# A trunk layer on one core: the output projection by seven products of quarters instead of eight blocks

## The chip, the core and the metric

The kernel runs on one core of a Trainium2 chip. A core has engines that each work through an instruction queue of their own, in order: TensorE (PE, matrix products; its weight loads are shown apart as PEld), VectorE (DVE), ScalarE (ACT), GpSimd (POOL) and SyncE (SP), which here issues nearly all the DMA transfers. They wait for one another through semaphores. The metric is the device time of one execution in microseconds (us); a run's median over several executions is compared.

## The reference, cut to what matters

One pre-norm residual layer on x of 512 rows and 1024 columns: a token mixer of three gated branches (attention, pooling, a state-space scan), an output projection, and a gated feed-forward block. The lines around the change are these:

```python
merged = gates[:, :, 0] * y_a + gates[:, :, 1] * y_b + gates[:, :, 2] * y_c
x = x + merged @ w_o[i]
x = x + conv_ffn(rmsnorm(x, ln2_g[i]), ffn_w_up[i], ffn_conv_w[i], ffn_conv_b[i], ffn_w_down[i])
```

`y_c` ends in a product with `w_c`; `merged @ w_o` is a 512 x 1024 by 1024 x 1024 product; the norm of its residual sum feeds the up projection `u @ w_up`. All is float32.

## The kernel before

**Products in three passes.** A float32 operand is split into a high part that TensorE can take (a cast on ScalarE, `cast`, L196) and the rest (a subtraction on VectorE, `lows`, L216). `mm3` (L237) adds high x high, high x low and low x high into one PSUM bank. For weights the parts are `wh` and `wl`, 128 x 2048 each for a 1 MB piece of weights; a piece arrives by one DMA on SP's queue (`fetch`, L184, tile `raw`, two buffers).

**Jobs.** The program is a list of jobs, each with one piece of weights. When job n starts, its instructions are recorded in this order: the split of job n+1 on VectorE, the cast of job n+2 on ScalarE (spread in halves over the job's steps), the fetch of job n+3 on SP, and then the job's own products and what takes their results. Each engine runs its instructions in exactly this recorded order. `step()` is called within a job; it flushes spread halves and moves on generators that wait in `running` (small pieces of other work, such as the transposes of a norm).

**Around the output projection.** Four jobs multiply by `w_c` (`branch_jobs` with `last=True`), two column chunks each, 24 matmuls of 128 x 512 per chunk. After chunk m, VectorE multiplies the result by its gate (L1162) and adds it to the merged sum `MG[m]` (L1163), ScalarE casts the sum (L1166, `mgh`) and VectorE takes the rest (L1167, `mgl`): 128 of the 1024 merged columns, for all 512 rows, are then ready as an operand.

`wo_jobs` forms the output: for each pair of row blocks (0, 1 and 2, 3), for each half h of the output columns, two jobs of four k blocks each. A job has two blocks of 12 matmuls, one per row block; a pair and half accumulates over two jobs in the same banks. So w_o is fetched, cast and split twice, once per pair: eight jobs of 24 matmuls. After the second job `evac` adds the bank to x (`X1[tb, h]`, L1188). For h = 0 `norm_early` starts the second norm (squares on ScalarE, L440; a product with the norm weights on GpSimd, L464); for h = 1 `norm_late` ends it (L472 square root, L474 to L482), and `norm_turn` transposes the normalised rows on TensorE (L453), with a cast (L456) and a split (L457) into `uh`, `ul`. The last two row blocks' norms run beside the first two up jobs (`opening`, L1356): high and low products of the first 256 rows, then one row block's transposes, then the product with `wl`.

PSUM has eight banks of 128 x 512, four with the tag "mm" and four with "sm". The columns of the up projection's convolution weights (`ff_cols`, tile `fcol`) are turned by two small transposes in this region.

**Products of quarters** stand in the kernel already, for two projections of the first stage (`sevens`) and for the down projection (`down_group`). There the left operand is cut in row halves (`LO`, `HI`) and in even and odd k blocks, the weights in k and column quarters, and seven products with sums of quarters replace eight. `sums_of` (L326 to L336) makes the sums of a pair of operand blocks: four 128 x 256 operations on VectorE, two casts on ScalarE, two splits on VectorE. `diff` (L341) subtracts one 128 x 2048 piece of weights from another. Two buffers of a pool (tile `w`, tag "xs") hold two quarters of weights; the first down group's pair is fetched there early, at the start of the w_c stage.

Of the kernel before, what the change touches and what calls it, by code (L numbers as in the profile page):

```python
# [10 lines left out]
F32 = mybir.dt.float32  # L11
F32R = mybir.dt.float32r
AF = mybir.ActivationFunctionType
# [70 lines left out]
def trunk(ctx: ExitStack, tc, out, x, rel_bias, ln1_g, w_in, b_gate, w_a, pool_w, pool_scale, w_b,  # L84
# [80 lines left out]
    def after(n, it):  # L165
        for _ in range(n):
            yield
        yield from it
# [57 lines left out]
    def wsrc(w, k0, k1, c0, c1):  # L226
        return w[k0 * P:k1 * P, c0:c1].rearrange("(k p) c -> p k c", p=P)

    def mm3(ps, wh, wl, xh, xl, ks, first=True, last=True, flip=False, onto=False):


        first = first and not onto
        n, total = 0, 3 * len(ks)
        for a, b in ((wh, xh), (wh, xl), (wl, xh)):
            for k in ks:
                l, r = (b(k), a(k)) if flip else (a(k), b(k))
                pe.matmul(ps, l, r, start=first and n == 0, stop=last and n == total - 1,  # L237
                          skip_group_check=onto)
                n += 1
# [82 lines left out]
    def sums_of(f0, f1, ah, al, found):  # L322


        sa, sb = T("sa"), T("sb")
        dve.tensor_tensor(sa[:, LO], f0[:, HI], f1[:, HI], OP.add)  # L326
        dve.tensor_tensor(sa[:, HI], sa[:, LO], f0[:, LO], OP.subtract)
        dve.tensor_tensor(sb[:, LO], f0[:, LO], f0[:, HI], OP.subtract)
        dve.tensor_tensor(sb[:, HI], f1[:, LO], sa[:, HI], OP.subtract)
# [5 lines left out]
        dve.tensor_sub(al, sa, ah.bitcast(F32))  # L335
        dve.tensor_sub(bl, sb, bh.bitcast(F32))  # L336
        for j, h, l, half in ((1, ah, al, LO), (2, ah, al, HI), (3, bh, bl, LO), (4, bh, bl, HI)):
            found(j, h[:, half], l[:, half])
# [117 lines left out]
            act.copy(hh, pv)  # L456
            dve.tensor_sub(ul[:, 4 * h:4 * h + 4, tb * P:(tb + 1) * P], pv, hh.bitcast(F32))  # L457
# [10 lines left out]
    def norm_late(t, g, v0, outs, last=False):  # L468
# [3 lines left out]
        act.activation(sq, ss, AF.Sqrt, bias=v0, scale=1.0 / D)  # L472
        xg = T("xg")
        dve.tensor_tensor(xg, t, g[:, S:], OP.mult)  # L474
        dve.scalar_tensor_tensor(v, ss, 1.0 / D, v0, OP.mult, OP.add)
        yield xg
        dve.reciprocal(r, sq)
        dve.scalar_tensor_tensor(rt, r, v, r, OP.mult, OP.mult)
        dve.tensor_scalar(rt, rt, -0.5, 1.5, OP.mult, OP.add)
        if not last:  # L480
            for o, src in outs(xg):
                dve.tensor_scalar(o, src, r, rt, OP.mult, OP.mult)  # L482
# [672 lines left out]
    def branch_jobs(b, w, parts, nk, last=False, more=()):  # L1155
        def evac(m, ps):
            if b == 1:
                MG[m] = T("yo")
                act.copy(MG[m], ps)
                return  # L1160
            s = SG[b, m]
            dve.tensor_tensor(s, s, ps, OP.mult)  # L1162
            (dve if last else pool).tensor_tensor(MG[m], MG[m], s, OP.add)  # L1163
            if last:
                h, l = T("mgh", F32R), T("mgl", F32R)
                act.copy(h, MG[m])  # L1166
                dve.tensor_sub(l, MG[m], h.bitcast(F32))  # L1167
                MH[m] = (h, l)

        return jobs_a(w, 0, 8, lambda k: parts[k][0], lambda k: parts[k][1], nk, evac,  # L1170
                      width=256 if nk > 4 else 512, more=more)


    X1 = {}
# [7 lines left out]
                t = X1[tb, h] = T("x1")  # L1182
                sp.dma_start(t, x[tb * P:(tb + 1) * P, h * S:(h + 1) * S])

    def wo_jobs(pair, h):
        def evac(tb, ps):
            t = X1[tb, h]
            dve.tensor_tensor(t, t, ps, OP.add)  # L1188
            if h == 0:
                nxt[tb] = norm_early(t, nxt["g2"])  # L1190
                return
# [5 lines left out]
            it = norm_late(t, nxt["g2"], v0, lambda xg1: ((us[0], xg0), (us[1], xg1)))  # L1197
            next(it)

            def rest():  # L1200
                next(it, None)
                yield
                norm_turn(us, nxt["uh"], nxt["ul"], tb)

            if pair == 0:
                r = rest()
                next(r)
                running.append(after(1, r))
# [8 lines left out]
        return jobs_b(lambda k0, k1: [wsrc(w_o, k0, k1, h * S, h * S + S)], S,  # L1217
                      lambda k, tb: MH[k][0][:, tb * P:(tb + 1) * P],
                      lambda k, tb: MH[k][1][:, tb * P:(tb + 1) * P], KD, evac,
                      blocks=(2 * pair, 2 * pair + 1), turn_over=pair == 1 and h == 1)  # L1220


    ACTS = {}
# [171 lines left out]
    def early(tb):  # L1395
        yield
        fin[tb] = norm_early(X1[tb, 0], fin["g"])
# [25 lines left out]
    def program():  # L1423
# [33 lines left out]
            else:  # L1457
                yield Call(lambda i=int(token): waiting.append(y_norm(i)))
        yield Call(finish)
        yield from branch_jobs(2, w_c, YT, 8, last=True)  # L1460
        yield Call(load_x1)
        for pair in range(2):
            for h in range(2):
                yield from wo_jobs(pair, h)
            if pair == 0:
# [235 lines left out]
```

## Time and profile before

| | |
|---|---|
| median of 3 runs | 1033.1 us (1032.99 to 1033.64) |
| the profiled execution | 1032.69 us |
| its span in the profile | 1030.9 us |
| TensorE busy | 1019.8 us, 5276 matmuls |
| VectorE, ScalarE, GpSimd busy | 702.7, 490.2, 132.8 us |
| w_c product | from 583.0 us |
| output projection | 626.5 to 672.3 us |
| opening of the up projection | 672.3 to 685.8 us |

Times of rows are from the span's start. A row of a group gives line, engine, operation, output <- inputs by tile names, the shape and the count; then busy us and mean ns of one; then the idle time of the engine just before these instructions and what ended it. A row of the timeline gives the start, the length, the engine and the operation, with the idle time before it in brackets. A row of several merged instructions counts from the start of the first to the end of the last. In the trace the tiles `X1` are called `x`, and the banks of the projection `pb`.

### The profile page before, as it was taken

How to read it: one execution, taken by the hardware profiler on the slowest of the kernel's cores; microseconds unless marked ns; L12 is line 12 of the kernel's file. 1: busy time of each engine (PE TensorE's matmuls, PEld its weight loads, DVE VectorE, ACT ScalarE, POOL GpSimd, SP SyncE). 2: the span in 40 equal slices, each digit the busy share in tenths (PEclk: the TensorE clock that was granted, in tenths of full speed). 3: DMA queues.
4: the chain of work that ended last, by engine and by line, in shares of the span. 5: the costliest groups of instructions: out<-in, count | busy, mean ns of one | idle time of the engine just before them, and what ended most of it. 6: DMA issues, size and time to landing. Idle time of an engine off the chain costs nothing.

```text
span 1030.9 us, 13254 instructions
## 1 busy us (share of the span) xinstructions
PE 1019.8 (99%) x5276; PEld 858.0 (83%) x5276; DVE 702.7 (68%) x932; ACT 490.2 (48%) x784; POOL 132.8 (13%) x114
## 2 busy tenths in 40 slices
PE   8999999999999999999999999999999999999997
PEld 8998877899888887788888888898888888888885
DVE  6553566788756648666688856767778668685756
ACT  6432545454674363567575324545444434433434
POOL 1770000000000001100044501101111100111002
PEclk9999999999999999999999999999999999999999
DMA  8444312034322354551253625543232233421322
GB/s 270 135 129 137 108 57 75 31 88 138 123 82 82 93 158 108 133 144 44 80 151 128 203 82 203 171 142 121 82 122 83 84 117 112 138 82 41 123 82 82
DMA packets 113357, 117.62 MB, mean 114 GB/s; under 512 B 5236, under 2 KB 97207, under 8 KB 113296
## 3 DMA queue, kind: packets, MB, share of 16 engines
q1 hardware_dynamic: 112703, 115.92, 36.4%
q8 instruction: 41, 0.67, 0.3%
q10 hardware_dynamic: 592, 0.86, 0.2%
q14 instruction: 21, 0.16, 0.1%
HBM read 112.97 MB, written 2.22 MB: 112 GB/s over the span
## 4 chain that ended last, share of the span: by engine, by line
PE 91%; DVE 4%; ACT 3%; issue 1%; DMA 1%; ACTq 0%; DVEq 0%
PE pa L237 30%; PE pu L237 22%; PE pb L237 12%; PE pd L237 7%; PE pqk L237 6%; PE pa L1552 2%; PE pq L237 2%; PE pu L1356 1%; PE ps L743 1%; PE pt L772 1%; PE ppw L237 1%; PE po L784 1%; DVE xs L1133 1%; DVE wl L216 1%; PE py L1057 1%
## 5 line engine op out<-in xcount | busy, mean ns | idle before, releaser
L216 DVE TENSOR_TENSOR wl<-raw,wh 128x2048 fp32r<-128x2048 f32 (+3 forms) x95 | 220.3, 2320 | 53.3 <-ACT wh L196 43.5
L196 ACT CAST wh<-raw 128x1024 fp32r<-128x1024 f32 (+3 forms) x188 | 187.6, 1017 | 48.3 <-DVE raw L341 18.0
L1251 DVE SCALAR_TENSOR_TENSOR hc<-pu,fcol,hc 128x510 f32<-128x510 f32 x88 | 65.8, 748 | 56.0 <-ACT hc L1248 54.4
L237 PE MATMUL pa<-uh,wh 128*128 128x512 f32 x384 | 98.4, 398 | 0.0
L237 PE MATMUL pa<-ul,wh 128*128 128x512 f32 x384 | 94.9, 389 | 0.0
L237 PE MATMUL pa<-uh,wl 128*128 128x512 f32 x384 | 94.8, 389 | 0.0
L237 PEld LDWEIGHTS pa<-ul,wh 128*128 128x128 f32 x384 | 72.1, 188 | 15.1
L237 PEld LDWEIGHTS pa<-uh,wl 128*128 128x128 f32 x384 | 72.1, 188 | 15.0
L237 PE MATMUL pu<-uh,wh 128*128 128x512 f32 (+1 forms) x352 | 83.6, 379 | 0.0
L237 PE MATMUL pu<-uh,wl 128*128 128x512 f32 (+1 forms) x352 | 83.5, 379 | 0.0
L237 PE MATMUL pu<-ul,wh 128*128 128x512 f32 (+1 forms) x352 | 83.5, 379 | 0.0
L237 PEld LDWEIGHTS pa<-uh,wh 128*128 128x128 f32 x384 | 70.3, 188 | 14.8 <-issue 1.0
L237 PEld LDWEIGHTS pu<-ul,wh 128*128 128x128 f32 x352 | 64.2, 188 | 12.5
L237 PEld LDWEIGHTS pu<-uh,wl 128*128 128x128 f32 x352 | 64.2, 188 | 12.5
L237 PEld LDWEIGHTS pu<-uh,wh 128*128 128x128 f32 x352 | 64.1, 188 | 12.4
L1248 ACT ACTIVATE hc<-pu,fcol,fcol 128x512 f32<-128x512 f32 x40 | 31.2, 780 | 80.5 <-PE pu L237 80.5
L1256 POOL TENSOR_TENSOR hc<-hc 128x512 f32<-128x512 f32 x22 | 30.8, 1402 | 289.1 <-DVE hc L1251 252.0
L1025 POOL TENSOR_TENSOR xd<-xc,dtz 128x512 f32<-128x512 f32 x6 | 6.4, 1063 | 355.9 <-issue 307.5
L765 ACT ACTIVATE sb<-sb,nmls 128x128 f32<-128x128 f32 (+1 forms) x72 | 30.1, 419 | 30.4 <-DVE nmls L762 17.7
L1149 ACT ACTIVATE sg<-pa,col 128x512 f32<-128x512 f32 x24 | 16.5, 688 | 45.5 <-PE pa L237 45.4
L1253 ACT ACTIVATE hc<-hc 128x512 f32<-128x512 f32 x22 | 13.9, 632 | 39.9 <-DVE hc L1251 39.9
L907 DVE SCALAR_TENSOR_TENSOR xs<-pa,col,xs 128x509 f32<-128x509 f32 (+2 forms) x24 | 18.0, 749 | 18.7 <-ACT xs L903 18.2
(373 smaller groups left out, 1868.0 us busy)
## 6 DMA issues: line engine op xcount, KB each, us to landing
raw<-in_w_in_dram SPq DMA_DIRECT2D x25, 1024.0 KB, 5.5
raw<-in_ffn_w_up_dram SPq DMA_DIRECT2D x22, 1024.0 KB, 5.2
raw<-in_w_o_dram SPq DMA_DIRECT2D x8, 1024.0 KB, 6.6
raw<-in_ffn_w_down_dram SPq DMA_DIRECT2D x8, 1024.0 KB
raw<-in_w_in_dram SPq DMA_DIRECT2D x14, 512.0 KB, 3.9
raw<-in_w_in_dram SPq DMA_DIRECT2D x6, 768.0 KB
raw<-in_w_b_dram SPq DMA_DIRECT2D x4, 1024.0 KB, 5.2
al<-ad SPq DMA_DIRECT2D x16, 256.0 KB, 7.7
```

The costliest lines, as they stand in the source:

```text
L196: act.copy(job.high[:, :, o], job.raw[:, :, o])
L216: (eng or dve).tensor_tensor(l[:, :, o], job.raw[:, :, o], h[:, :, o].bitcast(F32), OP.subtract)
L237: pe.matmul(ps, l, r, start=first and n == 0, stop=last and n == total - 1, skip_group_check=onto)
L743: pe.matmul(pss[i][:, o:o + w * P], q[r, n * P:(n + 1) * P], k[r, kb * P:(kb + w) * P], start=True, stop=True)
L765: act.activation(sb[:, off:off + w * P], sb[:, off:off + w * P], AF.Exp, bias=nm[:, n, h:h + 1], accum_out=ls[:, n, h:h + 1])
L907: dve.scalar_tensor_tensor(t[:, sh:], ps[:, :S - sh], col[:, o_cw + 12 * k + m:o_cw + 12 * k + m + 1], t[:, sh:], OP.mult, OP.add)
L1149: act.activation(s, ps, AF.Sigmoid, bias=col[:, o:o + 1])
L1248: act.activation(t, ps, AF.Identity, bias=ff["c1"][:, ff["b"] + m:ff["b"] + m + 1], scale=fw(2, m))
L1251: dve.scalar_tensor_tensor(t[:, sh:], ps[:, :S - sh], fw(k, m), t[:, sh:], OP.mult, OP.add)
L1253: act.activation(t, t, AF.Silu)
L1256: pool.tensor_tensor(a, a, t, OP.mult)
L1552: pe.matmul(first[2 * n + j][:, lo:hi], a[:, k, j * P:(j + 1) * P], b[:, k, lo:hi], start=a is wh and b is uh and k == 0, stop=a is wl and ...
```

## The change

`wo_group` takes the place of `wo_jobs`. The merged sum is the left operand: rows in halves (0 to 255, 256 to 511), the 128-column blocks as even and odd, so four pairs p of blocks 2p, 2p+1. `merged(m)` prepares them after chunk m of the w_c product: for even m it casts and splits only the first half of the rows (`mg0`); for odd m it casts and splits the whole block and runs `sums_of` on the pair, so that four sums (numbers 1 to 4, tiles `msh`/`msl` and `sbh`/`sbl`) are ready beside A11, A12 and A22.

The four quarters of w_o are fetched once: two into the "xs" pair `W` (the down projection's first pair is fetched after them), two as `raw` of the first two jobs. Seven jobs of two blocks follow; the table gives the left operand, the weights and the banks.

| job | left | weights | banks | results go to |
|---|---|---|---|---|
| one | A11 | quarter (0,0) | A | x of rows 0, 1, h = 0 |
| two | A12 | quarter (1,0) | two "sm" banks of its own | rows 0, 1, h = 0; first half of the norm |
| five | sum 1 | W[0], after a first difference | B | rows 2, 3, h = 1 |
| three | sum 4 | W[1] | B, on top | rows 0, 1, h = 1 |
| six | sum 2 | W[0], after a second difference | A, on top | rows 0, 1, h = 1; rest of the norm |
| seventh | sum 3 | raw of one, after a third | A, on top | rows 2, 3, h = 1; first half of the norm |
| four | A22 | raw of two, after a fourth | A, on top | rows 2, 3, h = 0; rest of the norm |

The first difference is recorded after the third w_c job, the others between the two blocks of jobs two, five and three. Each job adds its two banks to x, so there are 14 such adds for 8. `step()` runs after each block. A tiny square root (`wq`) after job two's second block loads ScalarE's table there. x is fetched before the last w_c job, the columns of `ff_cols` before job three.

In the built order VectorE's queue is, from the second difference on: add (two, block 1), split of three, add (five, block 0), third difference, add (five, block 1), split of six, add (three, block 0), fourth difference, add (three, block 1), split of seventh, add (six, block 0), and then the norms of the first two row blocks. On ScalarE the order there is: square of block 0, first half of three's cast, square of block 1, table load, `wq`, second half of three's cast.

```diff
-    def norm_early(t, g):
+    def norm_early(t, g, half=slice(0, S), steps=None):
...
-        dve.tensor_scalar(v0, ss, 1.0 / D, EPS, OP.mult, OP.add)
-        pool.tensor_tensor(xg, t, g[:, :S], OP.mult)
+        pool.tensor_tensor(xg, t, g[:, half], OP.mult)
+
+        def mean():
+            dve.tensor_scalar(v0, ss, 1.0 / D, EPS, OP.mult, OP.add)
...
+            steps.append(after(1, mean()))
...
             if last:
-                h, l = T("mgh", F32R), T("mgl", F32R)
-                act.copy(h, MG[m])
-                dve.tensor_sub(l, MG[m], h.bitcast(F32))
-                MH[m] = (h, l)
+                running.append(merged(m))
...
+    def merged(m):
+        a, p = MG[m], m // 2
+        if m % 2 == 0:
+            t = T("mg0", F32R)
+            act.copy(t[:, LO], a[:, LO])
+            dve.tensor_sub(t[:, HI], a[:, LO], t[:, LO].bitcast(F32))
+            MH[0, p] = (t[:, LO], t[:, HI])
+            return
+        h, l = T("mgh", F32R), T("mgl", F32R)
+        act.copy(h, a)
+        it = sums_of(MG[m - 1], a, T("msh", F32R), T("msl", F32R),
+                     lambda j, h, l: MH.__setitem__((j, p), (h, l)))
+        next(it)
+        dve.tensor_sub(l, a, h.bitcast(F32))
...
-    def wo_jobs(pair, h):
+    def wo_group():
...
+        def add(tb, h, ps):
+            dve.tensor_tensor(X1[tb, h], X1[tb, h], ps, OP.add)
+
+        def early(tb, h):
+            nxt[tb] = norm_early(X1[tb, h], nxt["g2"], slice(h * S, h * S + S), running)
+            if tb == 1:
+                act.activation(small("wq", [P, 1]), eps, AF.Sqrt)
...
+                for i in range(2):
+                    o = slice(i * P, (i + 1) * P)
+                    mm3(ps[i], lambda k: wh[:, k, :], lambda k: wl[:, k, :],
+                        lambda k: parts[k][0][:, o], lambda k: parts[k][1][:, o], range(4),
+                        flip=True, onto=more)
+                    use(i, ps[i])
+                    if i == 0 and between:
+                        between()
+                    step()
...
+        one = job("A11", quarter(0, 0), None, "A", lambda i, ps: add(i, 0, ps))
+        two = job("A12", quarter(1, 0), None, None, p2, between=lambda: diff(W[0], W[1], W[0]))
+        five = job(1, None, lambda: W[0], "B", lambda i, ps: add(2 + i, 1, ps),
+                   between=lambda: diff(one.raw, W[0], one.raw))
+        three = job(4, None, lambda: W[1], "B", lambda i, ps: add(i, 1, ps), more=True,
+                    between=lambda: diff(two.raw, two.raw, W[0]))
+        six = job(2, None, lambda: W[0], "A", p6, more=True)
+        seventh = job(3, None, lambda: one.raw, "A", p7, more=True)
+        four = job("A22", None, lambda: two.raw, "A", p4, more=True)
+        four.late = True
+        return load, lambda: diff(W[0], W[0], one.raw), [one, two, five, three, six, seventh, four]
...
-        yield from branch_jobs(2, w_c, YT, 8, last=True)
-        yield Call(load_x1)
-        for pair in range(2):
-            for h in range(2):
-                yield from wo_jobs(pair, h)
-            if pair == 0:
+        load, first, wo = wo_group()
+        yield Call(load)
+        for i, job in enumerate(branch_jobs(2, w_c, YT, 8, last=True)):
+            if i == 3:
+                yield Call(load_x1)
+            yield job
+            if i == 2:
+                yield Call(first)
+        for i, job in enumerate(wo):
+            if i == 3:
                 yield Call(ff_cols)
+            yield job
```

More of the change, by code (lines that the diff above doesn't have):

```diff
@@ L473, in norm_late @@
         xg = T("xg")
-        dve.tensor_tensor(xg, t, g[:, S:], OP.mult)
+        dve.tensor_tensor(xg, t, g[:, half], OP.mult)
         dve.scalar_tensor_tensor(v, ss, 1.0 / D, v0, OP.mult, OP.add)
@@ L1183, in load_x1, with load, finished @@
                 sp.dma_start(t, x[tb * P:(tb + 1) * P, h * S:(h + 1) * S])
-    def wo_jobs(pair, h):
[L1186 to L1191, printed above, removed]
+    def wo_group():
+        quarter = lambda two, h: w_o[:, h * S:(h + 1) * S].rearrange(
+            "(k two p) c -> two p k c", two=2, p=P)[two]
+        W, A, B = [], [], []
+        def load():
+            for two in range(2):
+                W.append(ypool.tile([P, 4, S], F32, name="w3", tag="xs"))
+                sp.dma_start(W[two], quarter(two, 1))
+        def add(tb, h, ps):
[4 more added lines that the diff above has]
+                act.activation(small("wq", [P, 1]), eps, AF.Sqrt)
+        def finished(tb, h):
             if "uh" not in nxt:
@@ L1203, in rest, with rest1 @@
                 norm_turn(us, nxt["uh"], nxt["ul"], tb)
-            if pair == 0:
-                r = rest()
-                next(r)
-                running.append(after(1, r))
+            if tb == 0:
+                running.append(after(1, rest()))
+            elif tb == 1:
+                def rest1():
+                    it = rest()
+                    next(it)
+                    yield
+                    yield
+                    yield from it
+                running.append(rest1())
             elif tb == 2:
@@ L1215, in evac, with job, body @@
                 late_split.pop(0)()
[L1217 to L1220, printed above, removed]
+        def job(j, raw, form, bank, use, more=False, between=None):
+            def body(ws):
+                wh, wl = ws
+                if not A:
+                    for b in (B, A):
+                        b.extend(MM("pb") for _ in range(2))
+                ps = {"A": A, "B": B}[bank] if bank else [SM("pb") for _ in range(2)]
+                if new.late:
+                    late_split.append(new.prepare(later=True))
+                parts = [MH[{"A11": 0}.get(j, j), p] for p in range(4)]
+                for i in range(2):
[7 more added lines that the diff above has]
+                    step()
+            new = Job([raw] if raw is not None else [], 4, S, body)
+            new.form = form
+            if raw is None:
+                new.load = lambda: None
+            return new
```

27 lines of the change are left out of this document (24 added, 3 removed).

## The prediction

> **What bounds the kernel now.** I read the page's busy line and chain first, then the busy time by stage around the output projection, then TensorE's timeline there.
>
> ```profile
> PE 1019.8 (99%) x5276; PEld 858.0 (83%) x5276; DVE 702.7 (68%) x932; ACT 490.2 (48%) x784; POOL 132.8 (13%) x114
> PE 91%; DVE 4%; ACT 3%; issue 1%; DMA 1%; ACTq 0%; DVEq 0%
> 583.00:626.50 43.50, 43.50 (x193) 36.02 (x192) 25.29 (x26) 11.02 (x14) 5.37 (x3) 1.00 0.35 114
> 626.50:672.30 45.80, 45.80 (x211) 37.92 (x211) 32.00 (x46) 24.12 (x38) 5.18 (x4) 1.00 0.58 202
> 672.30:686.00 13.70, 13.70 (x115) 13.48 (x115) 10.77 (x16) 6.84 (x11) 0.00 (x0) 1.00 0.57 187
> ```
>
> The stage rows (stretch, length, then busy PE, PEld, DVE, ACT, POOL, granted clock, DMA share, GB/s) are the w_c product, the output projection and the opening of the up projection. TensorE never waits in them; VectorE is busy 25.3 of 43.5 us, then 32.0 of 45.8 (70%), then 10.8 of 13.7.
>
> ```profile
> 624.74 1.98 PE L237 MATMUL pa<-yth,wl 128*128 128x512 f32 x8
> 626.55 1.07 PE L237 MATMUL pb<-wh,mgh 128*128 128x512 f32 x4
> 627.46 1.07 PE L237 MATMUL pb<-wh,mgl 128*128 128x512 f32 x4
> ...
> 676.20 1.04 PE L453 MATMUL uT<-eye,u 128*128 128x128 f32 x8
> 677.17 2.17 PE L1356 MATMUL pu<-uh,wl 128*128 128x256 f32 x16
> ...
> 683.81 2.15 PE L1356 MATMUL pu<-uh,wl 128*128 128x256 f32 x16
> 685.80 0.40 PE L237 MATMUL pu<-uh,wh 128*128 128x256 f32 x2
> ```
>
> Four matmuls go from 626.55 to 627.46: 0.227 us each, start to start. A block of 12 is 2.72, a job of two blocks 5.44. I carry the queues from 626.55 to the point that stands at 685.80; whatever that point moves, the end moves, as TensorE has no slack behind it.
>
> **The change, part by part.** *TensorE*: 8 jobs of 24 matmuls become 7: 24 x 0.227 = 5.44 us less, all on the path if nothing else waits. Transposes (32 + 2) stay.
>
> *VectorE*, from the rows (count, busy, mean ns; the first is of the projection's stretch alone):
>
> ```profile
> L216 DVE TENSOR_TENSOR wl<-raw,wh 128x2048 fp32r<-128x2048 f32 x7 | 15.9, 2290 | 4.0 <-ACT wh L196 3.9
> L341 DVE TENSOR_TENSOR w<-w,w 128x2048 f32<-128x2048 f32 x2 | 4.6, 2292 | 0.1
> L326 DVE TENSOR_TENSOR sa<-hc 128x256 f32<-128x256 f32 x8 | 3.3, 414 | 0.0
> L329 DVE TENSOR_TENSOR sb<-hc,sa 128x256 f32<-128x256 f32 x8 | 3.3, 419 | 0.0
> L335 DVE TENSOR_TENSOR sal<-sa,sah 128x512 fp32r<-128x512 f32 x12 | 8.2, 682 | 0.0
> L1188 DVE TENSOR_TENSOR x<-x,pb 128x512 f32<-128x512 f32 x8 | 5.5, 685 | 3.1 <-PE pb L237 3.1
> L1167 DVE TENSOR_TENSOR mgl<-yo,mgh 128x512 fp32r<-128x512 f32 x8 | 5.5, 693 | 5.5 <-ACT mgh L1166 5.5
> ```
>
> Four differences of weights 4 x 2.29 = 9.2; one split fewer -2.3; 16 quarter sums x 0.42 = 6.7; 8 splits of sums x 0.68 = 5.5; 14 adds into x for 8, 6 x 0.685 = 4.1; four of the eight mgl halved, 4 x 0.27 = -1.1. Together +22.1 us, of which only the first two pairs' sums fit in the w_c stage's idle 18 us at no cost. *ScalarE* gets 8 casts of sums and loses two weight casts, +2.4 us: cheap, but its order matters below. *SP*: w_o is read once (four loads for eight); W[0], W[1] take the two buffers in which the first down-projection weights were fetched early, so those loads now stand ahead of w_up's first in SP's queue. They are wanted only by the down groups, far behind; x is loaded earlier, harmless.
>
> Why VectorE then sets the pace: the adds free the banks. `three` accumulates onto `five`'s banks, `six` onto `one`'s, `seventh` onto `six`'s, `four` onto `seventh`'s; each block must wait until VectorE has added the earlier job's block, and in VectorE's fixed order a split or difference of 2.2 us lies between such adds. Hand-over rows:
>
> ```profile
> 658.80 2.28 DVE L216 TENSOR_TENSOR wl<-raw,wh 128x2048 fp32r<-128x2048 f32 x1
> 661.00 0.68 DVE L1188 TENSOR_TENSOR x<-x,pb 128x512 f32<-128x512 f32 x1
> 615.87 0.69 DVE L1162 TENSOR_TENSOR sg<-sg,pa 128x512 f32<-128x512 f32 x1 [2.58 <-PE pa L237]
> 583.83 3.38 DVE L216 TENSOR_TENSOR wl<-raw,wh 128x2048 fp32r<-128x2048 f32 x1
> 576.71 11.66 POOL L1163 TENSOR_TENSOR yo<-yo,sg 128x512 f32<-128x512 f32 x6 [1.23 <-DVE sg L1162]
> 646.51 0.63 ACT L440 ACTIVATE junk<-x 128x512 f32<-128x512 f32 x1 [3.64 <-DVE x L1188]
> 647.05 0.18 ACT L440 ACTIVATION_READ_ACCUMULATOR junk<-x 128x1 f32 x1
> 647.25 1.28 ACT L472 ACT_TABLE_LOAD   x1
> 648.55 0.29 ACT L472 ACTIVATE sq<-ss,v 128x1 f32<-128x1 f32 x1
> 652.18 1.03 ACT L196 CAST wh<-raw 128x1024 fp32r<-128x1024 f32 x1
> ```
>
> A split takes 2.20 start to start, an add about 0.61. VectorE is on time at 615.87 (sixth w_c chunk). From there, in the built order:
> 1. sg, yo, two splits of pair 1, four quarter sums, mgl to 620.7; the first difference and `one`'s split to 625.2; chunk 6 (ready 621.3) to 627.5; chunk 7, pair 2's splits, pair 3's sums, mgl to 632.3; `two`'s split to 634.5. `two` starts at 626.55 + 5.44 = 632.0, wants it at 633.8: wait 0.7.
> 2. Two adds of `one`, two splits, `five`'s split to 639.1 (needed 640.0); add of `two` block 0 to 639.8; second difference. Beside it GpSimd multiplies x by the norm weights. The row at 583.83 shows a split beside GpSimd at 3.38 instead of 2.29; I take +1.0 here (ends 0 and 1.1, taking the row like it). Difference to 642.9, add of `two` block 1 to 643.6.
> 3. `three`'s split needs the second half of its cast, and ScalarE's order puts before that the square of block 1 (which needs the add just made), the table load and a square root: 643.6 + 0.54 + 0.20 + 1.30 + 0.5, cast 1.04, = 646.8. VectorE idles 3.2; the split ends at 649.1; `five`'s first add at 649.7. `five` was over at 643.6: TensorE waits **6.1**. This is the largest term.
> 4. Third difference, add, `six`'s split, add, fourth difference, add, `seventh`'s split, to 660.5; `three` and `six` run within that, without waits. Add of `six` block 0 to 661.1, `seventh` starts.
> 5. Two norms of the first row blocks end at 665.0 (u0) and 667.0. TensorE wants u0 after `seventh` block 0: wait 1.1. `four`'s split to 669.2, add to 669.9: `four` waits 0.4.
> 6. ScalarE now casts half of w_up's first weights and the transposes, with squares between; VectorE waits 2.2 us twice (ul2 at 672.0 and 676.1), and block 1 of `four` waits 1.3 for an add that stands behind the first two. `four` ends at 676.6.
> 7. The opening products run; row block 2's norm is ready at 680.9 (wait 0.4); the split of w_up's first weights ends only at 684.6, so the wl product that stood at 677.17 starts at 684.7 (wait 2.9).
>
> Durations in 5 to 7 are these:
>
> ```profile
> L474 DVE TENSOR_TENSOR xg<-x,grow 128x512 f32<-128x512 f32 x8 | 5.5, 692 | 0.3
> L482 DVE TENSOR_SCALAR u<-xg,r,rt 128x512 f32<-128x512 f32 x8 | 4.0, 544 | 0.4
> L457 DVE TENSOR_TENSOR ul<-uT,uh 128x512 fp32r<-128x512 f32 x8 | 5.0, 683 | 2.6 <-ACT uh L456 2.6
> L456 ACT CAST uh<-uT 128x512 fp32r<-128x512 f32 x8 | 4.2, 586 | 0.0
> ```
>
> Waits: 0.7 + 6.1 + 1.1 + 0.4 + 1.3 + 0.4 + 2.9 = 12.9; less 5.44: +7.5 us. The profiled execution takes 1032.7 (span 1030.9 and 1.8 around it), 0.4 under the median; 1033.1 + 7.5 = 1040.6 for the median.
>
> The table load is weighed once. The load starts 0.02 us after the accumulator read ends, and 1.30 lies between it and the square root. [...]
>
> **Rivals.** *The saving shows (faster).* With no wait of TensorE's it would be 1033.1 - 5.4 = 1027.7. For it: VectorE is idle 30% of the stretch. Against it: the +22 us, bunched behind 615.9. VectorE's work from there to 684.6 holds about 9 us of waits for ScalarE (0.6, 3.2, 2.2, 2.2, the rest small); had it none, that split would end at 675.7, which is 1.4 ahead of 677.1. So the mechanism is ScalarE's casts coming early enough, it decides below about 1.5 us of such waits, and gives about 1031.7 at best.
>
> *W_up late.* The two down-projection loads (1 MB each) can go only after the fourth difference, at 657.6, and the first w_up load after `seventh`'s split, at 660.5:
>
> ```profile
> 620.00:630.00 10.00, 10.00 (x46) 8.29 (x45) 5.82 (x8) 3.31 (x5) 0.00 (x0) 1.00 0.75 254
> 630.00:640.00 10.00, 10.00 (x46) 8.29 (x45) 6.15 (x6) 4.11 (x8) 2.59 (x2) 1.00 0.73 271
> ```
>
> 3.15 MB at 271 GB/s land at 669.3, in time for ScalarE's cast at 670.5; at the projection's mean 202 at 673.2, 2.7 late, and the transposes' casts stand behind it: 1043.3.
>
> *The clock falls.* After the 6.1 us wait TensorE might run at a lower pace. One block at half pace is 2.7 us more; VectorE's lag hides about half of it by `six` block 1: +1.3, 1041.9.
>
> ```profile
> 6.90 2.05 PE L1569 MATMUL uT<-diag,xin 128*128 128x128 f32 x16 [1.28 <-DVE diag L1581]
> 4.00:8.00 4.00, 2.72 (x21) 2.53 (x21) 2.55 (x11) 2.01 (x7) 0.00 (x0) 1.00 1.09 331
> ```
>
> Here a gap of 1.28 us left the granted clock at 1.00; no longer one is in the trace. [...]
>
> **How the numbers follow.** Forecast as summed (within 2.5 us): 0.62. W_up late: 0.10, about 1043. Clock down: 0.13, about 1042. Both end by 1046. Waits for ScalarE partly gone, 1034 to 1038: 0.07. Faster: 0.05; the rest, near no change, 0.03. Without the GpSimd overlap the sum is 1039.6, and each us of ScalarE wait less is one us the other way; with late weights and clock both it is 1044.6. So 1036.5 to 1045.5, which leaves out some 2 in 10. A difference under 0.2% (2 us), about what a measurement of this kernel can tell from no change, counts as none. Faster 0.05, same 0.03, slower 0.92.
>
> **What would show it.** Right: TensorE's waits name the add (L1223) with one near 6 us before `three`, then the up projection's split; VectorE waits about 3 us for a cast ahead of `three`'s split; the table load stands between them; the w_c stage is unchanged. Wrong: no wait of TensorE over 2 us in the projection; VectorE idle there above 20%; or a wait that names a DMA.

## The result, and the profile after

The changed kernel takes 1041.83 us (median; 1040.05 to 1041.96) against 1033.11 (1032.81 to 1033.64) for the kernel before beside it, 8.7 us more. The ratio, which is taken over all the runs and so isn't quite that of the medians, is 1.0079, 95% interval 1.0066 to 1.0092. The profiled execution takes 1040.35 us, 7.66 over the profiled one of before, and all readings below are of that one. (The runs of the changed kernel fall into two groups, at 1040.05 and 1040.35 and at 1041.72 to 1041.96; the profile is of the lower.)

The page's span, busy line and chain of the changed kernel:

```profile
span 1038.2 us, 13237 instructions
PE 1018.1 (98%) x5252; PEld 854.7 (82%) x5252; DVE 720.6 (69%) x965; ACT 492.8 (47%) x791; POOL 134.6 (13%) x114
PE 86%; DVE 8%; ACT 4%; issue 1%; DMA 1%; ACTq 0%; DVEq 0%
```

TensorE has 24 matmuls fewer, VectorE is busy 17.9 us longer (the time in which its instructions overlap is counted once), and VectorE's share of the chain has doubled. Busy time by stage (stretch, length, then busy PE, PEld, DVE, ACT, POOL, granted clock, DMA share, GB/s):

```profile
583.00:626.50 43.50, 43.50 (x194) 36.02 (x193) 32.08 (x42) 13.61 (x20) 5.31 (x3) 1.00 0.40 135
626.50:680.00 53.50, 47.10 (x213) 37.80 (x212) 43.11 (x63) 23.81 (x40) 7.05 (x4) 0.94 0.24 80
646.00:651.00 5.00, 2.81 (x7) 2.26 (x8) 5.00 (x6) 1.66 (x3) 0.00 (x0) 0.51 0.38 133
651.00:656.00 5.00, 5.00 (x20) 4.01 (x19) 4.67 (x3) 1.35 (x2) 0.00 (x0) 0.80 0.21 80
```

The w_c stage is as long as before. In the projection TensorE, which never waited there, is busy 47.1 of 53.5 us; VectorE is busy 43.1 of them. The last two rows show something more: the granted clock is 0.51 and 0.80 about where `three` begins. TensorE's waits from 580 to 720 us (what waited, for whom; us in total, times, longest):

```profile
PE pb L237 <- DVE x L1223: 6.1, 3, 4.8
PE pu L1451 <- DVE wl L216: 2.6, 1, 2.6
PE uT L453 <- DVE v L466: 0.2, 1, 0.2
PE uT L453 <- DVE u L491: 0.2, 1, 0.2
```

Every one is for VectorE, none for a DMA. They stand in TensorE's timeline (start, length, instruction, count, idle time before it) as follows:

```profile
632.84 1.07 PE L237 MATMUL pb<-wh,mgl 128*128 128x512 f32 x4
633.98 1.20 PE L237 MATMUL pb<-wl,mgh 128*128 128x512 f32 x4
...
648.19 2.04 PE L237 MATMUL pb<-wh,sbh 128*128 128x512 f32 x4 [4.84 <-DVE x L1223]
650.03 1.91 PE L237 MATMUL pb<-wh,sbl 128*128 128x512 f32 x4
651.74 1.66 PE L237 MATMUL pb<-wl,sbh 128*128 128x512 f32 x4
653.24 1.07 PE L237 MATMUL pb<-wh,sbh 128*128 128x512 f32 x4
...
674.03 1.20 PE L237 MATMUL pb<-wh,mgh 128*128 128x512 f32 x4 [1.06 <-DVE x L1223]
...
684.83 2.17 PE L1451 MATMUL pu<-uh,wl 128*128 128x256 f32 x16 [2.65 <-DVE wl L216]
...
693.47 1.12 PE L237 MATMUL pu<-uh,wh 128*128 128x256 f32 x8
```

The point that stood at 685.80 stands at 693.47. Before `three` TensorE idles 4.84 us, and then its first block takes 5.05 us (648.19 to 653.24) in place of 2.72. Now VectorE, ScalarE and GpSimd ahead of that wait, from their timelines:

```profile
639.04 2.28 DVE L341 TENSOR_TENSOR w<-w,w 128x2048 f32<-128x2048 f32 x1
641.25 0.68 DVE L1223 TENSOR_TENSOR x<-x,pb 128x512 f32<-128x512 f32 x1
...
645.15 2.29 DVE L216 TENSOR_TENSOR wl<-w,wh 128x2048 fp32r<-128x2048 f32 x1 [3.16 <-ACT wh L196]
641.96 0.63 ACT L440 ACTIVATE junk<-x 128x512 f32<-128x512 f32 x1 [1.13 <-DVE x L1223]
642.50 0.19 ACT L440 ACTIVATION_READ_ACCUMULATOR junk<-x 128x1 f32 x1
642.69 1.28 ACT L1228 ACT_TABLE_LOAD   x1
643.98 0.20 ACT L1228 ACTIVATE wq<-eps 128x1 f32<-128x1 f32 x1
644.09 2.92 ACT L196 CAST wh<-w 128x1024 fp32r<-128x1024 f32 x3
639.27 4.46 POOL L463 TENSOR_TENSOR xg<-x,grow 128x512 f32<-128x512 f32 x2 [50.96 <-DVE x L1223]
```

This is the prediction's step 3 in rows: add, square, accumulator read, table load, square root, and only then the cast (the first of the three merged in that row) for which VectorE's split of `three` has waited 3.16 us.

### The profile page after: what moved, and what is told of

It reads as the page before. It is cut to its first block, busy times and chain, and to the rows that moved or that the text cites. A ratio compares the mean times of both kernels' runs of the same rounds, so it can differ in the third digit from the quotient of the medians.

```text
span 1038.2 us, 13237 instructions
## 1 busy us (share of the span) xinstructions
PE 1018.1 (98%) x5252; PEld 854.7 (82%) x5252; DVE 720.6 (69%) x965; ACT 492.8 (47%) x791; POOL 134.6 (13%) x114
## 4 chain that ended last, share of the span: by engine, by line
PE 86%; DVE 8%; ACT 4%; issue 1%; DMA 1%; ACTq 0%; DVEq 0%
PE pa L237 28%; PE pu L237 22%; PE pb L237 10%; PE pd L237 7%; PE pqk L237 6%; PE pa L1652 2%; PE pq L237 2%; DVE wl L216 2%; PE ps L752 1%; PE pt L781 1%; PE ppw L237 1%; PE po L793 1%; ACT wh L196 1%; DVE xs L1142 1%; PE pu L1451 1%
## 5 line engine op out<-in xcount | busy, mean ns | idle before, releaser
L216 DVE TENSOR_TENSOR wl<-raw,wh 128x2048 fp32r<-128x2048 f32 (+3 forms) x91 | 211.2, 2321 | 48.1 <-ACT wh L196 39.4
L196 ACT CAST wh<-raw 128x1024 fp32r<-128x1024 f32 (+3 forms) x180 | 180.0, 1016 | 59.0 <-DVE raw L341 18.0
L216 DVE TENSOR_TENSOR wl<-w,wh 128x2048 fp32r<-128x2048 f32 (+1 forms) x15 | 32.2, 2146 | 5.1 <-ACT wh L196 5.1
```

The costliest lines, as they stand in the source:

```text
L196: act.copy(job.high[:, :, o], job.raw[:, :, o])
L216: (eng or dve).tensor_tensor(l[:, :, o], job.raw[:, :, o], h[:, :, o].bitcast(F32), OP.subtract)
```

## The experiments

Theory A is the prediction's: VectorE runs in a fixed order, ScalarE's casts come late in its own, and each bank is freed only when VectorE gets to its add. Rival B: VectorE's added work sets the time, whatever its order. Theory C: TensorE's clock falls where it idles, and that adds to each long wait. The medians stand in one table; each ratio is to the kernel before, run beside it, over all runs of both.

| | edit | median, us | ratio, 95% interval |
|---|---|---|---|
| after | | 1041.83 | 1.0079 (1.0066 to 1.0092) |
| 1 | cast of `three` ahead of the square | 1038.11 | 1.0057 (1.0044 to 1.0070) |
| 2 | table load earlier | 1039.84 | 1.0067 (1.0054 to 1.0080) |
| 3 | 40 small products before `three` | 1043.87 | 1.0104 (1.0089 to 1.0119) |
| 4 | no late differences | 1039.92 | 1.0072 (1.0059 to 1.0084) |
| 5 | 20 small products before `three` | 1042.32 | 1.0088 (1.0074 to 1.0101) |
| 6 | 1, 2 and `four`'s split behind an add | 1036.34 | 1.0035 (1.0021 to 1.0049) |
| 7 | 6, and up weights' split ahead of an add | 1033.16 | 0.9999 (0.9991 to 1.0008) |
| 8 | 7, and first difference earlier | 1032.71 | 1.0000 (0.9991 to 1.0008) |
| 9 | 8, and a square behind the casts | 1031.44 | 0.9985 (0.9976 to 0.9994) |
| 10 | 9, and four sums on GpSimd | 1031.45 | 0.9984 (0.9975 to 0.9992) |
| 11 | 9, and 8 small products before `three` | 1031.35 | 0.9982 (0.9973 to 0.9991) |

### 1. The second half of `three`'s cast ahead of the square of block 1

```diff
                     if i == 0 and between:
                         between()
+                    if i == 0 and j == "A12":
+                        flush()
                     step()
```

> Only ScalarE's order changes: both halves of three's weight cast stand before the square of two's block 1 and the table load. Theory A (VectorE's fixed order, held up by where ScalarE's casts stand): the 3.2 us for which VectorE waits for that cast go, TensorE's wait before three falls from 4.8 to about 2 us, the block behind it runs at full pace, and the whole falls by 3.2 + 1.3 = 4.5 us, to about 1037.3. Rival B (the amount of VectorE's work alone): the wait only moves to the next adds, under 1 us is gained, above 1040.8. Rival C (only the slow block behind the wait costs): 1.3 us, about 1040.5.

1038.11 us, 3.7 under after; A's 1037.3 is missed by 0.8. TensorE's timeline of this kernel, at `three` and at the first up product with wl:

```profile
645.43 1.17 PE L237 MATMUL pb<-wh,sbh 128*128 128x512 f32 x4 [2.02 <-DVE x L1223]
...
680.93 3.38 PE L1453 MATMUL pu<-uh,wl 128*128 128x256 f32 x16 [2.66 <-DVE wl L216]
684.10 2.40 PE L1453 MATMUL pu<-uh,wh 128*128 128x256 f32 x16
```

The wait before `three` is 2.02 in place of 4.84 and its block runs at full pace (granted clock 1.00 over 646 to 651 us), with the same work on every engine: order makes that wait. What is missing of the forecast stands in the other rows: after 2.66 us of waiting the product with wl takes 3.17 us (680.93 to 684.10) in place of 2.01, and the next one is slow too. In after's profile that product waited as long and then ran at full pace (684.83 to 686.84).

### 2. The table load two jobs earlier

```diff
-            if tb == 1:
-                act.activation(small("wq", [P, 1]), eps, AF.Sqrt)
...
+                if j == "A11":
+                    act.activation(small("wq", [P, 1]), eps, AF.Sqrt)
```

> The tiny square root with its table load moves to the start of job one, where ScalarE is idle; the cast's place behind block 1's square stays. Theory A: the table load and the root leave the chain of the cast, 1.6 us earlier, wait before three 3.3 us; 1.6 less if the next block still runs slowly, 2.9 less if it does not: 1038.9 to 1040.2. Rival B: no change, 1041.8.

1039.84, within A's range. VectorE's split of `three` in this kernel:

```profile
643.62 2.29 DVE L216 TENSOR_TENSOR wl<-w,wh 128x2048 fp32r<-128x2048 f32 x1 [1.66 <-ACT wh L196]
```

1.66 in place of 3.16: the load and its square root (1.40 us from 642.69 to the cast at 644.09 in after) are gone from ScalarE's path there, and the wait before `three` is 1.5 shorter, 3.34.

### 3 and 5. Small products in the wait

```diff
+                if j == 4:
+                    idle = SM("fill")
+                    for _ in range(40):
+                        pe.matmul(idle[:, :P], ones.bitcast(F32), ones.bitcast(F32), start=True, stop=True)
```

The fifth experiment has 20 for 40.

> 40 small products (128 columns, about 0.11 us each) on a bank of their own stand between five and three, so that TensorE works through most of the 4.8 us wait; all else stays. If the slow block after the wait comes from TensorE's idling, block 0 of three takes 2.72 us instead of 5.05, and the end comes some 1.3 us earlier, about 1040.5, with single runs within 0.5 us of each other. If the slow block has another cause, it stays and the time is unchanged or a little longer.

> After, with 20 small products on a spare bank ahead of `three`, so half as many as in the third experiment (there 9.09 us for the 40; here about 4.5, inside the 4.84 us that TensorE waits). They compute nothing that is used. Theory that idling TensorE lowers the clock: the first block of `three` takes 2.7 to 2.9 us in place of 5.05, VectorE's lag takes back about 1 us of that, and the wait before the up projection's wl product stays near 2.7, with the clock falling behind it in some runs: 1039.5 to 1041, at best 1 us under after. Rival, that the slow block comes from what runs beside it (VectorE and ScalarE busy, the second half of the cast) and not from the wait: the block stays near 5 us and the time at after's 1041.8.

TensorE's timeline of the fifth:

```profile
643.68 4.62 PE L1277 MATMUL fill<-ones 128*128 128x128 f32 x40
648.64 1.17 PE L237 MATMUL pb<-wh,sbh 128*128 128x512 f32 x4 [0.34 <-DVE x L1223]
...
651.49 1.12 PE L237 MATMUL pb<-wh,sbh 128*128 128x512 f32 x4
...
683.65 3.78 PE L1455 MATMUL pu<-uh,wl 128*128 128x256 f32 x16 [2.65 <-DVE wl L216]
687.23 3.11 PE L1455 MATMUL pu<-uh,wh 128*128 128x256 f32 x16
```

Two of this kernel's stage rows, at `three` and at the product with wl:

```profile
646.50:651.50 5.00, 4.66 (x30) 3.87 (x28) 5.00 (x6) 1.66 (x3) 0.00 (x0) 1.00 0.48 142
681.50:686.50 5.00, 2.85 (x13) 2.85 (x14) 4.84 (x9) 2.88 (x5) 0.00 (x0) 0.63 0.59 204
```

`three` starts at 648.64, 0.45 later than in after, as do the blocks ahead of the wait, but its first block takes 2.85 us (648.64 to 651.49) in place of 5.05, and the granted clock is 1.00 there. VectorE and ScalarE do beside it what they did, so the slow block came from TensorE's idling: C holds here. The medians did not fall (1042.32; 1043.87 for the 40, whose 80 records of 9.09 us overran the wait), so both experiments miss what was expected of the time (about 1040.5, and 1039.5 to 1041). The product with wl does start 1.2 us earlier than in after (683.65), but in this execution the clock fell behind that wait, to 0.63: 3.58 and 2.95 us, start to start, for products of 1.9 to 2.0 us, 2.6 us together. The gain at `three` did not reach the end.

### 4. Without the three differences between blocks

```diff
-        two = job("A12", quarter(1, 0), None, None, p2, between=lambda: diff(W[0], W[1], W[0]))
+        two = job("A12", quarter(1, 0), None, None, p2)
```

and so for `five` and `three`.

> Leaves out the three differences of weights between the blocks of two, five and three, so six, seventh and four multiply by other weights; the work of TensorE, ScalarE and the DMAs stays. 3 x 2.2 = 6.6 us of VectorE's work go. Rival B (amount of VectorE's work): all of it comes off, about 1035.2. Theory A: the cast of three still stands behind block 1's square and the table load, and the later waits for casts stay; only about 3.7 us come off, about 1038.1, and VectorE's wait for three's cast grows from 3.2 to about 3.9 us.

1039.92. Three operations of 2.28 us less on VectorE, and only 1.9 us less in the median; B's 1035.2 falls, A's 1038.1 is closer. VectorE of this kernel:

```profile
644.07 2.29 DVE L216 TENSOR_TENSOR wl<-w,wh 128x2048 fp32r<-128x2048 f32 x1 [3.85 <-ACT wh L196]
```

VectorE reaches the split earlier and waits for the cast longer, 3.85 in place of 3.16; the wait before `three` is still 3.59. A's number is missed by 1.8. The profiled execution, one of 1041.26 us, shows what could make this up: two products behind the later 2.65 us wait took 3.58 and 2.96 us, which is 2.6 too long (granted clock 0.73 and 0.59 over 680 to 685 and 685 to 690 us), where after's profile lost nothing (1.00 in both).

### 6. Three moves of order at once

Experiments 1 and 2, and `seventh`'s call of its preparation (the split for `four`) after its first add:

```diff
-                if new.late:
+                if new.late and not new.turn:
                     late_split.append(new.prepare(later=True))
...
+                    if i == 0 and new.turn:
+                        new.prepare()
...
+            new.turn = new.late = j in TURN
...
+TURN = (3,)
```

> After, with three moves of order and no work less: the second half of `three`'s cast ahead of the square of block 1 (first experiment), the square root's table load two jobs earlier (second experiment), and the split for `four` behind `seventh`'s... first add, not ahead of it. Theory A, that VectorE's fixed order and ScalarE's cast order make the waits: carried through the queues, the up projection's point comes 6.8 us ahead of after's, so about 1033.6 by after's profiled 1040.35, with a wait of about 2.7 us left before the wl product and up to 1.5 us more where the clock falls behind it: 1033 to 1035.5. Rival B, that the added VectorE work alone sets the time and the order only shifts the waits: no better than the first experiment, 1037 to 1038.5.

1036.34: below B's range, 0.8 above A's. Timeline of TensorE:

```profile
645.54 1.66 PE L237 MATMUL pb<-wh,sbh 128*128 128x512 f32 x4 [2.03 <-DVE x L1223]
647.00 1.91 PE L237 MATMUL pb<-wh,sbl 128*128 128x512 f32 x4
648.70 1.41 PE L237 MATMUL pb<-wl,sbh 128*128 128x512 f32 x4
...
679.33 3.17 PE L1456 MATMUL pu<-uh,wl 128*128 128x256 f32 x16 [2.65 <-DVE wl L216]
682.30 2.62 PE L1456 MATMUL pu<-uh,wh 128*128 128x256 f32 x16
```

Here the clock fell twice: granted 0.71 over 646.5 to 651.5 us, 0.86 and 0.80 over the two stretches of 5 us from 676.5 to 686.5. The first block takes 4.41 us (645.54 to 649.95, where the next one starts), 1.7 too long, though the wait before it was only 2.03; the two products behind the second wait lose 1.5. The waits for `four` (0.24 and 1.06 in after) are gone.

### 7. The split of the first up weights ahead of `four`'s second add

```diff
             elif tb == 2:
                 r2 = rest()
                 next(r2)
                 late.append(r2)
+                late_split.pop(0)()
             else:
                 late.append(rest())
-                late_split.pop(0)()
```

> The sixth experiment's kernel with the split of the first up weights moved ahead of `four`'s second add on VectorE. Theory A: the wait before the wl product falls from about 2.7 to about 1.2 us and the clock no longer falls behind it: 1032 to 1033.5, level with before. Rival: `four`'s second block then waits for the add that is moved back by 2.2 us, and the gain is lost: no change from the sixth experiment.

1033.16, within A's range and level with before. TensorE of this kernel:

```profile
677.01 2.17 PE L1456 MATMUL pu<-uh,wl 128*128 128x256 f32 x16 [1.04 <-DVE v L466]
```

The 2.65 us wait is 1.04 and the product behind it runs at full pace (2.01 us to the next, granted clock 1.00 over 676.5 to 681.5 us). Moving one 2.28 us operation by one place took 3.2 us off the median. In the profiles 1.6 of it is the wait, and the 1.5 lost behind the wait is gone; but the 1.7 lost at `three` in the sixth's profile is absent from this one too, so how much of the 3.2 us is the clock's isn't shown.

### 8. The first difference one w_c job earlier

```diff
-            if i == 2:
+            if i == 1:
                 yield Call(first)
```

> The seventh experiment's kernel with the first difference one job earlier in the w_c stage, where VectorE has idle time. Theory A: the backlog with which VectorE enters the projection falls by up to 2.3 us, of which 0.6 to 0.7 reaches the end, since the other waits are ScalarE's: 1031.3 to 1032.5, faster than before by about 0.1%. Rival: the difference falls in the way of the w_c job's own splits and TensorE waits in that stage: 1033 or more.

1032.71, 0.2 above A's range and below the rival's. The medians of 7 and 8 are 0.45 apart and the intervals of both take in no change: not a gain that the runs tell from none. VectorE of this kernel, at the last w_c chunk:

```profile
627.66 0.69 DVE L1171 TENSOR_TENSOR sg<-sg,pa 128x512 f32<-128x512 f32 x1 [1.29 <-PE pa L237]
```

VectorE, freed of 2.2 us, idles 1.29 of them here, and the wait before `three` stays at 2.02. The price put on the backlog was too high.

### 9. A square behind the casts it held up

Row block 3's square waits for VectorE's add of `seventh`'s second block, and on ScalarE stood ahead of the casts of row block 1's transposes.

```diff
         def p7(i, ps):
             add(2 + i, 1, ps)
-            early(2 + i, 1)
+            if i:
+                running.append(last_early())
+            else:
+                early(2, 1)
```

`last_early` makes the same square and product one generator later.

> The eighth experiment's kernel with one edit in ScalarE's order: the square of row block 3 (it waits for VectorE's add of `seventh`'s second block) stands behind the casts of row block 1's transposes, not ahead of them. Theory A, that this square is why VectorE idles 2.21 us ahead of the second ul split: that idle time goes, the split of the first up weights ends about 2 us earlier, the wait before the wl product (1.04 us) goes, and so does what is left behind it; carried through the queues the up projection's point comes 1.5 us earlier: 1031 to 1031.8, 0.1 to 0.2% under before. Rival: the casts then wait for TensorE's transposes, or the first half of the mean comes too late for row block 3's norm, and the wait moves on: no change from 1032.7.

1031.44, 0.9985 (0.9976 to 0.9994): within A's range, and faster than the kernel before by the interval, though 1.7 us is less than the 0.2% that the prediction counts as a difference. VectorE and TensorE of this kernel:

```profile
668.03 1.29 DVE L457 TENSOR_TENSOR ul<-uT,uh 128x512 fp32r<-128x512 f32 x2
...
672.73 2.29 DVE L216 TENSOR_TENSOR wl<-raw,wh 128x2048 fp32r<-128x2048 f32 x1
675.85 2.15 PE L1466 MATMUL pu<-uh,wl 128*128 128x256 f32 x16
```

The second ul split no longer waits (2.21 in after), the weights' split ends at 675.0, and the wl product starts with no wait. What is left of TensorE's waits is 2.04 and 0.28 before `three`'s two blocks and 0.71 before the first transposes: 3.0 us and some tenths behind each, of the 5.44 that the change takes away.

### 10. The last pair's sums on GpSimd

```diff
-                     lambda j, h, l: MH.__setitem__((j, p), (h, l)))
+                     lambda j, h, l: MH.__setitem__((j, p), (h, l)),
+                     pool if m == 7 else dve)
```

with the engine handed on to `sums_of`.

> The ninth experiment's kernel with the four sums of the last pair of merged chunks on GpSimd (idle there) in place of VectorE. Theory A, that VectorE's backlog out of the w_c stage is what `three` still waits for (2.02 us): VectorE is rid of four ops of 0.42 us, 1.4 us start to start, the wait falls to 0.5 to 0.8, TensorE's clock stays at 1.00 behind it, and the end comes 1.0 to 1.4 us earlier: 1029.6 to 1030.8, 0.2 to 0.35% under before. Rival: GpSimd, held up beside VectorE, delivers the sums late (needed by `five` about 10 us after the last chunk), and TensorE waits there in place of `three`: 1031 or more.

1031.45: no gain, a miss for A's 1029.6 to 1030.8, and not as the rival had it either. VectorE beside those sums, the last of the sums, and TensorE at `three`:

```profile
628.25 0.68 DVE L336 TENSOR_TENSOR msl<-sa,msh 128x512 fp32r<-128x512 f32 x1
628.85 1.23 DVE L337 TENSOR_TENSOR sbl<-sb,sbh 128x512 fp32r<-128x512 f32 x1
630.00 1.23 DVE L1195 TENSOR_TENSOR mgl<-yo,mgh 128x512 fp32r<-128x512 f32 x1
631.15 2.83 DVE L216 TENSOR_TENSOR wl<-raw,wh 128x2048 fp32r<-128x2048 f32 x1
631.79 2.78 POOL L330 TENSOR_TENSOR sb<-yo,sa 128x256 f32<-128x256 f32 x1
645.43 1.33 PE L237 MATMUL pb<-wh,sbh 128*128 128x512 f32 x4 [2.01 <-DVE x L1225]
```

Beside GpSimd two of VectorE's operations took 1.23 in place of 0.68 and the split 2.83 in place of 2.28: 1.65 us lost where 1.46 (629.74 to 631.20 in the ninth) were moved away. `three` waited 2.01, as before, and in this profile its first block ran slowly behind that (4.42 us, granted clock 0.66 over 646 to 651 us).

### 11. Eight small products in the wait that is left

The edit of the third experiment with `range(8)`, on the ninth's kernel.

> The ninth experiment's kernel with 8 small products on a spare bank ahead of `three`, in the 2.04 us wait that is left there (by the 4.62 us for 20 of them in the fifth experiment, 1.85 us; nothing of them is used). If the idle time there lowers the clock in some executions (it did behind waits of 2.01 to 2.03 us in the profiles of the sixth, eighth and tenth experiments, not in those of the first, seventh and ninth), the spread of the ninth experiment's runs (1030.75 to 1032.13) closes towards its low end: median 1030.8 to 1031.1, the highest run under 1031.6. If the run-to-run spread has another cause: median 1031.4 and the same spread.

1031.35, the high end further down (1031.94 for 1032.13) and the low end further up (1031.08 for 1030.75): the second reading is nearer. The clock does fall behind this wait in some executions (0.66 over 646 to 651 us in the profiles of the sixth, eighth and tenth, 1.00 in those of the first, seventh and ninth), but part of the slow block is time that TensorE waits for VectorE otherwise: the wait before the first transposes is 0.71 in the ninth's profile, without the fall, and 0.18 in the tenth's, with it. If a mean granted clock of 0.996, as in the tenth's profile, marks the fall, the ninth's runs with it average 1031.28 and the others 1031.55, so it doesn't seem to be what spreads them; what does stays open.

## Why the prediction was right

The forecast of 1040.6 us lies 1.2 under the median; the +7.5 it carried for the point before the up projection measured +7.7 in the profiled execution, and 1041.83 lies in its range. The mechanism is the forecast's: waits for VectorE's adds and splits, the longest of them made by ScalarE's order. That the number came so near is in part luck, as the errors of the sum cancel: the waits were put too long, and the slow products behind them at nothing. Of the signs named, the waits and their causes came; but the longest wait was 4.84 for "near 6", and VectorE's idle share of the projection, 10.4 of 53.5 us or 19%, lies only just under the 20% that was to count against the forecast.

- **TensorE saves 5.44.** 5252 matmuls for 5276; the blocks that wait for nothing have the old spacing.
- **VectorE gets +22.1.** Right as a sum of lengths: over the three stages the lengths of its instructions come to about 92 us for 70. Its busy time grew by 17.9 only, as instructions that follow one another overlap by 0.09 (2.29 long, 2.20 start to start) and busy time counts that once.
- **Step 1, `two` waits 0.7.** Too large: the product with `two`'s wl starts 1.14 us after the one before it (632.84, 633.98) in place of 0.91, and loses another 0.12 at its start: 0.35.
- **Step 2, the second difference is held up by GpSimd, +1.0.** Wrong. It took 2.28 us, and GpSimd was held up instead: its two products took 4.46 together where the later ones take 1.29 each. The split at 583.83, from which the 1.0 was taken, began while GpSimd was already at work (576.71 to 588.37); here the difference began first. The first experiment shows both cases: its GpSimd products run from 639.32 to 645.83, the difference begun at 639.09 took 2.29, the split begun at 641.96 took 2.73.
- **Step 3, `three` waits 6.1.** The chain is right to the row (VectorE's wait 3.2 forecast, 3.16 measured), and experiments 1 and 2 show each link. The wait is 4.84, mostly since step 2's 1.0 did not come; but the block behind it lost 2.33 to the clock, which the sum had at nothing, and a rival, given a chance of 0.13, at 2.7. 6.1 was forecast, 7.2 measured.
- **Step 4, no waits.** Right.
- **Step 5, 1.1 and 0.4.** 0.19 and 0.24: TensorE came later out of `three`, and VectorE had caught up.
- **Step 6, VectorE waits 2.2 twice, `four` waits 1.3.** 2.27, 2.21 and 1.06.
- **Step 7, 0.4 and 2.9.** 0.23 and 2.65.

The waits and the slow block come to 0.35 + 4.84 + 2.33 + 0.19 + 0.24 + 1.06 + 0.23 + 2.65 = 11.9, less 5.44 is 6.5; the other 1.2 is a tenth to a quarter of a us by which the products behind each wait start late or run long, which the steps did not count.

**The rivals.** W_up was not late. SP's queue and ScalarE's cast of the first half:

```profile
647.47 9.31 SPq L1399 DMA_DIRECT2D w<-in_ffn_w_down_dram  x2
659.15 10.47 SPq L184 DMA_DIRECT2D raw<-in_ffn_w_up_dram  x2
670.55 1.03 ACT L196 CAST wh<-raw 128x1024 fp32r<-128x1024 f32 x1
```

The down projection's two loads go at 647.47 and 656.39 (both 657.6 in the forecast), w_up's first at 659.15 (660.5 forecast), and the cast waits for no transfer. That the clock falls was a rival, and it came, behind a shorter wait: the wait and the slow block cost 7.2 together where the forecast had 6.1 and this rival, with half of the slow block hidden, 7.4. Its 1041.9 lies nearer to the median than the 1040.6 of the forecast. The half pace that it took for one block is in no row of before; after's block took 5.05 us for 2.72, with a granted clock of 0.51 over 646 to 651 us, and those of experiments 2, 4, 6, 8 and 10 took 4.15 to 4.42. That the saving shows, if ScalarE's casts come early enough, was put at about 1031.7 at best; with six changes of order the ninth experiment gives 1031.44. The bound was about right, and the decision did lie with ScalarE's casts and with the order of VectorE's adds.

**The table load.** The load starts 0.00 us after the accumulator read ends (642.69) and the square root 0.01 after the load (643.98 against 643.97): nothing lies beside the 1.28, and what the second experiment took off the wait, 1.5 us, is about the 1.40 from the load to the next cast.

**What stays open.** The sum says nothing of the upper group of runs. A fall of the clock behind the 2.65 us wait would make such a difference (1.5 to 2.6 us in other profiles, none in after's), but no profile of a run of that group was taken, and the mean clocks of after's runs do not sort them.

## What to carry to other kernels

When work on the bound engine is traded for work on another, sum the traded work at the places where banks and buffers change hands, in the queues' recorded order: here the price was made by what stood ahead of an add or a cast, and six moves of order together won 10.4 us with no work taken away (of the fifth, the first difference, the runs show no gain by itself). Look on the helping engine for instructions that wait for something late (a square that needs an add, a table load) ahead of casts that others need now. And an idle gap of TensorE can cost more than its length: here waits of 2 us and more were followed in 12 of 16 cases by slow products, which cost 1.4 to 2.6 us more.

## What the runs showed of the hardware that was not expected

**The clock falls after short waits, in some executions.** Behind waits of 1.08 us and less the products run at full pace in every profile (behind 1.04, in 7 and 8, with a granted clock of 1.00 over 676.5 to 681.5 us). Behind waits of 2.01 to 2.04 us (`three`, experiments 1, 6, 7, 8, 9, 10) they ran slow in three profiles and at full pace in three. Behind 2.65 and 2.66 us (the wl product) they ran at full pace in after's and slow in those of experiments 1 to 6; behind 3.34 us and more, slow in each. (The wl product's wait follows 1.06 us of transposes, `three`'s follows full products, so the two waits aren't quite the same case.) The blocks and products that ran slowly take 4.15 to 6.5 us in all, 1.4 to 2.6 too long. The granted clock over 646 to 651 us, about where `three` begins, was 0.51 in after's profile, 0.66 to 0.71 in those of 2, 4, 6, 8 and 10, and 1.00 in those of 1, 7 and 9; over 680 to 695 us, with the wl product, 1.00 in after's and 0.77 to 0.89 in those of 1 to 6. What differs from execution to execution after equal waits, no run shows.

**VectorE and GpSimd beside each other.** They held each other up: GpSimd's two products (the later ones of after take 1.29 and 1.30) took 4.46 us begun just behind a difference of weights, and 6.51 with a split beside the second (first experiment); VectorE lost 0.45 to 0.55 us on an operation begun while GpSimd was at work, and 1.1 in the split at 583.83 of the kernel before. So moving four sums to an idle GpSimd gained nothing: VectorE lost 1.65 us for the 1.46 that it was spared.

**The small float32 products count twice.** 20 products of 128 x 128 x 128 in plain float32 show as 40 records and take 4.62 us, 0.23 us each (fifth experiment); the 40 of the third show as 80 and take 9.09.
